# Seven block products for eight in the key and query projections of a hybrid GLA and dilated-window trunk, with low parts added by transfers

## The chip, the cores and the metric

The kernel runs on one core of one Trainium2 chip, as one program. The metric is the device time in microseconds, from the first to the last instruction with what lies around them, as the median of several runs. Engines are named as in the profile: PE is TensorE's matmuls, PEld its weight loads, DVE the VectorE, ACT the ScalarE, POOL the GpSimd and SP the SyncE, which in the kernel before issues all DMA transfers.

## The reference, cut to what matters

A sequence of 1024 tokens with 1024 features goes through two layers. The first is gated linear attention. The second is attention in dilated windows: three groups g with windows of 128, 512 and 2048 tokens at steps of 1, 4 and 16, two key heads c that four query heads each share, and one gate g. The change touches the second layer's projections and how its attention is fed:

```
def shared_kv(x, w_kv):
    kv = x @ w_kv
    k, v = jnp.split(kv, [SWA_KV_HALF], axis=-1)
    k = rope(k.reshape(bsz, s, SWA_N_GROUPS * SWA_KV_HEADS, SWA_HEAD_DIM), pos)
...
def dilated_mixer(x, w_in, w_out, k_sh, v_sh):
    proj = x @ w_in
    q, g = jnp.split(proj, [SWA_Q_TOTAL], axis=-1)
    q = rope(q.reshape(bsz, s, SWA_N_GROUPS * SWA_Q_HEADS, SWA_HEAD_DIM), pos) * (SWA_HEAD_DIM ** -0.5)
    for gi, (window, dilation) in enumerate(SWA_GROUPS):
        o_g, lse_g = dilated_window_attention(q[:, :, gi], k_sh[:, :, gi], v_sh[:, :, gi], window, dilation)
    wts = jax.nn.softmax(jnp.stack(lses, axis=0), axis=0)
    o = jnp.sum(wts[..., None] * jnp.stack(outs, axis=0), axis=0)
    return (o.astype(x.dtype) * jax.nn.silu(g)) @ w_out
...
x = layer_norm(DEEPNORM_ALPHA * x + y, ln_g[layer], ln_b[layer])
```

## The kernel before

**Precision.** Every fp32 product is made of three matmuls in fp32r, a format with a shorter mantissa. A number is split into a high part (`split_hi`, a copy to fp32r) and a low part (`split_lo`, the number less its high part), and `mm3` (L642) adds high by high, high by low and low by high. Tiles with h at the end of their name are high parts, those with l low parts.

**Projections.** `project` (L655) makes one tile of 128 output columns by 1024 tokens: `load_w` (L625) brings 512 KB of weights by SP into `wf` (2 buffers), ACT writes the high part to `wh` (3 buffers), DVE or POOL the low part to `wl` (3 buffers). Then 48 matmuls follow, two halves of 512 tokens by 8 blocks of features by 3. The inputs are x1h and x1l, eight pairs of pages of 128x1024.

**Order of the program.** `layer_a` (from L725) is the first layer. `out_ln` makes its output projection and layer norm for one half of the tokens after the other, and hands on the x1 tiles. `layer_b` (from L1176) then does the following.

1. `proj_v(0)` and `proj_v0` for the first half of the tokens: values for groups 1 and 2, and for group 0.
2. The loop at L1267 to L1270: six key tiles `wK` by `project`, each with `rope` (a product with cosT, two with sinT on 64 rows each, and a sum), and `rows`, which turns one block of x1 through TensorE for the end.
3. `proj_v(1)`, the other values, and the spill of the second key head to DRAM (`kvd`, from L1277).
4. Eight units u, one per query head (loop from L1512): `scores(u)` with masks and exponentials, sums `sts` that go through DRAM and come back turned (`std`, `nat`), the weights of the three groups (`cwd`, `cw`), `q_proj(u + 1)` with three query tiles, `attend(u)`, and the gate tile `g_proj` (L1310) with its product in `close` (L1504). All transfers in this are issued by SP. `reload_kv` brings the second key head after unit 3.
5. `out_ln` and `out_ln_rows` (L1579 to L1595): the output projection and layer norm of the second layer. For the first half of the tokens it is `early()`, within the last units.

**What sets the order.** Nothing is issued where it is written. A list scheduler `Sched` (order from L254, cost from L543) records all operations, estimates each one's time and writes out a fixed order for each engine. `S.later(-WEIGHTS)` lets weight loads go first, `S.later(-EVAC)` lets results leave PSUM early, and an operation given as `S.vp` goes to DVE or POOL, whichever the scheduler finds free first. All instructions are issued at one line (L452 before, L454 after), so they are told apart by tiles. PSUM has four tags of two banks each: acc, lv, po, ms.

Of the kernel before, what the change touches and what calls it, by code (L numbers as in the profile page):

```python
# [7 lines left out]
F32 = mybir.dt.float32  # L8
# [28 lines left out]
RUNS, GATHER = 0.3, 1.0  # L37

# [102 lines left out]
class Sched:  # L141
# [20 lines left out]
    def record(self, engs, meth, args, kw):  # L162
# [10 lines left out]
        if meth == "copy_predicated":  # L173
            ins += outs
# [79 lines left out]
    def order(self):  # L254
# [26 lines left out]
        dma_free = 0.0  # L281
# [35 lines left out]
        while n_done < len(ops):  # L317
# [43 lines left out]
            if e == "SP":  # L361
                dma_free = max(dma_free, st) + c
                o.t1 = dma_free + 1.7
                free[e] = st + 0.37
# [167 lines left out]
def shares_port(e, meth, outs, ins):  # L532

    n = sum(v.buf.pool.space is None for v in ins if int(_np.prod(v.shape[1:])) > 1)
    if e == "POOL":
        return n > 0
# [6 lines left out]
def cost(e, meth, n, outs, ins, args, kw):  # L543
# [14 lines left out]
    if e == "SP":  # L558
        return 0.1 + int(_np.prod((outs + ins)[0].shape)) * 4 / 280e3
# [38 lines left out]
def trunk(tc, xT, wP, wA, wA12, wAv3, w2, wO, wK, wV0, wV12, wB, wOB, par_d,  # L598
# [5 lines left out]
    p0 = S.pool("p0")  # L604
    ps = S.pool("ps", space="PSUM")
# [14 lines left out]

    def hs(half):
# [3 lines left out]
    def load_w(src):  # L625
        with S.later(-WEIGHTS):
            return load_w_now(src)

    def load_w_now(src):
# [9 lines left out]
        split_lo(lo, wf, hi)  # L639
# [15 lines left out]
    def project(piece, xs, evac, halves=(0, 1)):  # L655
        w = load_w(piece)
# [68 lines left out]
    def layer_a(t2, t1, after):  # L725
        lmask = t2.tile([128, NLEV - 2, 32], U8, name="lmask")
        smask = t2.tile([128, 512], F32, name="smask")
# [155 lines left out]
        def gate(h):  # L883
            b = t1.tile([128, T], F32, name="b", tag="b", bufs=2)
            H[h]["b"] = b
            for half in range(2):
# [10 lines left out]
                S.vector.tensor_tensor_scan(b[:, r], smask, mn, 0.0, op0=OP.mult, op1=OP.add)  # L897
# [256 lines left out]
    kvd = [dram.tile([128, T], F32, name=f"kvd{i}") for i in range(4)]  # L1154
# [21 lines left out]
    def layer_b(xs, early):  # L1176
# [12 lines left out]
        cosT = page(p0, F32, "cosT")  # L1189
        S.sync.dma_start(cosT, cos_d)  # L1190
        sinT = page(p0, F32, "sinT")
        S.sync.dma_start(sinT, sin_d)

        def rope(pg, g, half, acc):
# [8 lines left out]
        K = [[page(p0, F32, f"K{c}{g}") for g in range(3)] for c in range(2)]  # L1203
        V = [[None] * 3 for _ in range(2)]

        def proj_v0(blocks):
            for c in range(2):
                if V[c][0] is None:
                    V[c][0] = page(p0, F32, f"V{c}0")

            def evac(j, acc):
                S.scalar.activation(blk(V[0][0], j), acc[:, 0:128], AF.Copy)
                S.vector.tensor_copy(blk(V[1][0], j), acc[:, 128:256])
            project_tok(wV0, xs, [(j, lambda x, j=j: blk(x, j)) for j in blocks], evac)

        def proj_v(half):
# [12 lines left out]
            with S.later(-EVAC):  # L1231
                pgs = [page(p0, F32, "Vn") for _ in range(2)]
# [24 lines left out]
        def rows(et):  # L1257
            f, t = small("x1f", "d", 4), small("x1r", "d", 4)
# [5 lines left out]

        proj_v(0)
        proj_v0(range(4))
        for g in range(3):  # L1267
            for c in range(2):
                project(wK[2 * g + c], xs, lambda hf, acc, p=K[c][g]: rope(p, g, hf, acc))
                rows(2 * g + c)  # L1270
        proj_v(1)
        for g in (1, 2):
            load_v(0, g)
        rows(6)
        rows(7)
        proj_v0(range(4, 8))
        for g in range(3):  # L1277
            S.sync.dma_start(kvd[g], K[1][g])
        S.sync.dma_start(kvd[3], V[1][0])

        def reload_kv():
            for g in range(3):
                K[1][g] = page(p0, F32, f"K1{g}")
                S.sync.dma_start(K[1][g], kvd[g])
            V[1][0] = page(p0, F32, "V10")
            S.sync.dma_start(V[1][0], kvd[3])
            load_v(1, 1)
            load_v(1, 2)


# [12 lines left out]
        def q_proj(u):  # L1303
            Q = [page(p0, F32, "Q") for _ in range(3)]
            U[u]["Q"] = Q
            for g in range(3):
                project(wB[u, g], xs, lambda half, acc: rope(Q[g], g, half, acc))


        def g_proj(u):  # L1310
            sg = page(p0, F32, "sg")
            U[u]["sg"] = sg
# [373 lines left out]
```

## Time and profile before

| | us |
|---|---|
| median of 3 runs | 1154.0 |
| lowest and highest run | 1153.88, 1154.59 |
| span of the profiled execution | 1152.7 |
| PE busy in it | 1142.8 |
| DVE busy | 820.3 |
| ACT busy | 449.1 |
| POOL busy | 188.0 |

Busy times are sums over the instructions of an engine, and the page gives them as shares of the span. The windows of the trace show the same for a stretch, the chain of waits follows the work that ended last back to the start, and groups by form give the mean duration of one instruction of a shape. In a group the number after x is the count, then come the busy time, the mean in ns, and the idle time ahead of it with what ended it. Of the page's issues, these are the ones that the change moves or adds to, with their count and size:

```profile
wf<-in_wB SPq DMA_DIRECT2D x32, 512.0 KB
...
wf<-in_wK SPq DMA_DIRECT2D x6, 512.0 KB
```

The first are the weights of the 24 query tiles and 8 gate tiles, the second those of the six key tiles.

### The profile page before, as it was taken

Reading aid. Unit: us, or ns where it says so; the run is one execution under the profiler, and the core shown is the slowest. Engines: PE = TensorE matmul, PEld = TensorE weight load, DVE = VectorE, ACT = ScalarE, POOL = GpSimd, SP = SyncE. Lnnn points to the kernel's source line nnn. Section 1 sums busy time; section 2 is a strip of 40 time slices with the busy share of each in tenths; the row PEclk is TensorE's granted clock in tenths of the full one; section 3 lists DMA queues with packets and bytes.
Section 4 is the critical chain, followed back from the end, with each engine's and each line's share of the span. In section 5 each row is a group of like instructions: output and inputs, shape, how many; then the busy total and the mean of one; then the engine's idle time right before and its main releaser. Section 6 shows DMA issues by size and latency. Waiting matters only on the chain.

```text
span 1152.7 us, 19731 instructions
## 1 busy us (share of the span) xinstructions
PE 1142.8 (99%) x7780; PEld 975.2 (85%) x7780; DVE 820.3 (71%) x1634; ACT 449.1 (39%) x929; POOL 188.0 (16%) x139
## 2 busy tenths in 40 slices
PE   9999999999999999999999999999999999999997
PEld 9888888889988888888988888888888888888876
DVE  6286862786966699764366868686777878767678
ACT  5355431646463335311214242424222443444342
POOL 1000100112011120211020303030211312212200
PEclk9999999999999999999999999999999999999999
DMA  7211222111144365443611111121141111134544
GB/s 256 71 38 38 74 79 87 38 61 51 57 171 140 137 214 158 166 143 103 208 47 34 51 38 57 38 50 45 38 165 39 38 21 38 39 96 126 193 136 182
DMA packets 93372, 108.39 MB, mean 94 GB/s; under 512 B 43648, under 2 KB 61952, under 8 KB 93280
## 3 DMA queue, kind: packets, MB, share of 16 engines
q1 hardware_dynamic: 93280, 107.13, 29.6%
q8 instruction: 61, 1.00, 0.4%
q14 instruction: 31, 0.25, 0.1%
HBM read 85.94 MB, written 21.17 MB: 93 GB/s over the span
## 4 chain that ended last, share of the span: by engine, by line
PE 93%; DVE 4%; DMA 2%; ACT 1%; issue 1%; POOL 0%; DVEq 0%; ACTq 0%
PE acc L452 63%; PE po L452 9%; PE lv L452 8%; PE vac L452 7%; PE ms L452 4%; PE pro L452 2%; DMA wf<-in_wOB 2%; DVE rt L452 1%; DVE wl L452 1%; DVE x1l L452 0%; ACT wh L452 0%; DVE P L452 0%; DVE lnA L452 0%; ACT woh L452 0%; DVE wol L452 0%
## 5 line engine op out<-in xcount | busy, mean ns | idle before, releaser
L452 PE MATMUL acc<-x1h,wh 128*128 128x512 f32 x608 | 252.3, 415 | 0.0
L452 PE MATMUL acc<-x1h,wl 128*128 128x512 f32 x608 | 237.6, 391 | 0.0
L452 PE MATMUL acc<-x1l,wh 128*128 128x512 f32 x608 | 237.1, 390 | 0.0
L452 ACT ACTIVATE wh<-wf 128x1024 fp32r<-128x1024 f32 (+2 forms) x104 | 108.1, 1040 | 281.0 <-PE acc L452 194.8
L452 POOL TENSOR_TENSOR wl<-wf,wh 128x1024 fp32r<-128x1024 f32 x39 | 93.5, 2397 | 553.1 <-ACT wh L452 414.8
L452 ACT ACTIVATE P<-P,sts 128x128 f32<-128x128 f32 (+2 forms) x192 | 81.5, 426 | 139.6 <-DVE sts L452 139.3
L452 PEld LDWEIGHTS acc<-x1h,wl 128*128 128x128 f32 x608 | 114.1, 188 | 24.5
L452 PEld LDWEIGHTS acc<-x1l,wh 128*128 128x128 f32 x608 | 114.5, 188 | 21.3
L452 PEld LDWEIGHTS acc<-x1h,wh 128*128 128x128 f32 x608 | 114.4, 188 | 21.1
L452 DVE TENSOR_TENSOR wl<-wf,wh 128x1024 fp32r<-128x1024 f32 (+2 forms) x66 | 83.4, 1265 | 58.2 <-ACT wh L452 48.0
L452 PE MATMUL acc<-xh,wh 128*128 128x512 f32 x256 | 101.8, 397 | 0.0
L452 PE MATMUL acc<-xh,wl 128*128 128x512 f32 x256 | 99.8, 390 | 0.0
L452 PE MATMUL acc<-xl,wh 128*128 128x512 f32 x256 | 99.7, 390 | 0.0
L452 DVE TENSOR_TENSOR t<-acc,cosT 128x512 f32<-128x512 f32 x60 | 41.4, 689 | 65.7 <-PE acc L452 65.7
L452 DVE TENSOR_TENSOR t<-acc,sinT 64x512 f32<-64x512 f32 x120 | 82.5, 688 | 1.6
L452 PE MATMUL lv<-K,Q 128*64 128x64 f32 (+2 forms) x512 | 70.2, 286 | 0.0
L452 DVE CUSTOM_DVE_ANT_0 P<-lv,bmask 128x256 f32<-128x256 f32 (+1 forms) x128 | 46.7, 379 | 25.1 <-PE lv L452 23.7
L452 PEld LDWEIGHTS lv<-K,Q 128*128 128x128 f32 (+1 forms) x512 | 53.8, 163 | 10.0 <-issue 1.6
L452 PE MATMUL acc<-ogh,wh 128*128 128x512 f32 x152 | 60.1, 395 | 0.0
L452 PE MATMUL acc<-ogh,wl 128*128 128x512 f32 x152 | 59.2, 389 | 0.0
L452 PE MATMUL acc<-ogl,wh 128*128 128x512 f32 x152 | 59.2, 389 | 0.0
L452 PEld LDWEIGHTS acc<-xh,wl 128*128 128x128 f32 x256 | 48.0, 188 | 10.2
(252 smaller groups left out, 2233.4 us busy)
## 6 DMA issues: line engine op xcount, KB each, us to landing
wf<-in_wB SPq DMA_DIRECT2D x32, 512.0 KB
wf<-in_wA SPq DMA_DIRECT2D x24, 512.0 KB
wf<-in_wO SPq DMA_DIRECT2D x16, 512.0 KB
wf<-in_wOB SPq DMA_DIRECT2D x16, 512.0 KB
wf<-in_wV SPq DMA_DIRECT2D x12, 512.0 KB
res<-in_xT SPq DMA_DIRECT2D x16, 256.0 KB
x1d<-rt SPq DMA_DIRECT2D x16, 256.0 KB
out<-rt SPq DMA_DIRECT2D x16, 256.0 KB
```

Of the source, the lines that this page charges most:

```text
L452: getattr(handle[o.eng], meth)(*[conv(a) for a in args], **{k: conv(v) for k, v in kw.items()})
```

## The change

**Seven products.** Two tiles of 128 columns that read the same x1 form a matrix product of two by two blocks: two tiles by two halves of the features for the weights, two halves of the features by two halves of the tokens for x1. Eight block products, each of 4 x 3 matmuls of 128x512, give the four results. The change uses the scheme with seven: P1 to P7, with four sums of weight blocks (built by `load_pair`) and four sums of x1 blocks, T1 to T4 (built by `sums`, 16 pages of 128x1024). Nine pairs go this way: the three pairs of key tiles, and 12 of the 24 query tiles by the list EARLY, all of it ahead of attention. The results, and the values of group 0, are stored to DRAM (`kd`, `qd`, `vd0`) and loaded when a unit needs them.

```
EARLY = [(0, 1, 2), (2, 3, 2), (0, 2, 1), (4, 5, 2), (6, 7, 2), (4, 6, 1)]
...
                def put(w, x, more=None):
                    hi, lo = w
                    split_hi(hi, x)
                    S.scalar.activation(lo, x, AF.Copy, scale=-1.0)
                    if more is None:
                        S.gpsimd.dma_start(lo, x, accum_op=OP.add)
                    else:
                        S.gpsimd.dma_start(four(lo), more, accum_op=OP.add)
                    return four(hi), four(lo)
...
                w0, w1 = halves()
                a11 = put(w0, a[:, L], src[0][:, 0:4])
                t3 = total(S.vp.tensor_sub, a[:, L], b[:, L])
                s3 = put(w1, t3)
                w0, w1 = halves()
                a12 = put(w0, a[:, R], src[0][:, 4:8])
                a22 = put(w1, b[:, R], src[1][:, 4:8])
                w0, w1 = halves()
                t1 = total(S.vp.tensor_add, b[:, L], b[:, R])
                s1 = put(w0, t1)
                t2 = total(S.vp.tensor_sub, t1, a[:, L])
                s2 = put(w1, t2)
                t4 = total(S.vp.tensor_sub, a[:, R], t2)
                s4 = put([small("s4", "d", 4, FR) for _ in range(2)], t4)
            return dict(P1=a11, P2=a12, P4=a22, P7=s3, P5=s1, P6=s2, P3=s4)
...
        def seven(w, evac):
...
            acc = prod("P1", "a")
            u = small("u1", "a", 13)
            with S.later(-WEIGHTS - EVAC):
                S.scalar.copy(u, acc)
            acc = prod("P7", "b")
            f = small("u2", "a", 13)
            with S.later(-WEIGHTS - EVAC):
                S.scalar.copy(f, acc)
            acc = prod("P2", "a")
            with late():
                evac(0, 0, acc)
            prod("P4", "b")
            acc = prod("P5", "c")
            with late():
                S.vector.tensor_add(f, f, acc)
            acc = prod("P6", "d")
            with late():
                S.vector.tensor_add(u, u, acc)
                c21 = small("c", "a", 13)
                S.vector.tensor_add(c21, u, banks["b"])
                evac(1, 0, c21)
                S.vp.tensor_add(f, u, f)
                evac(1, 1, f)
            acc = prod("P3", "c")
            with late():
                S.vector.tensor_add(u, u, acc)
                evac(0, 1, u)
...
        def sums():
            for k in range(4):
                t, low = raws[k], raws[k + 4]
                old, old2 = (small("old", "d", 4) for _ in range(2))
                S.sync.dma_start(old, x1d[k][:, 0:512])
                S.sync.dma_start(old2, x1d[k + 4][:, 0:512])
                S.vp.tensor_sub(old, t, old)
                keep("T1", k, old)
                S.vp.tensor_sub(t, low, t)
                keep("T3", k, t)
                S.vp.tensor_sub(low, low, old)
                keep("T2", k, low)
                S.vp.tensor_sub(old2, old2, low)
                keep("T4", k, old2)
```

The order of `layer_b` ahead of attention becomes proj_v(0), proj_v0, proj_v(1), proj_v0, sums, nine pairs.

**Low parts by transfers.** In a pair, and in `q_proj` and `g_proj` (`added=True`), the low part is no longer a subtraction on DVE or POOL. ACT writes the negated high-precision number to wl, in fp32r, and a DMA that POOL issues adds the number itself to it: 63 such transfers of 256 KB and 20 of 512 KB.

```
-        split_lo(lo, wf, hi)
+        if added:
+            S.scalar.activation(lo, wf, AF.Copy, scale=-1.0)
+            S.gpsimd.dma_start(lo, src, accum_op=OP.add)
+        else:
+            split_lo(lo, wf, hi)
```

**Rope.** Two copies on ACT and one product take the place of two products on DVE, and the sign in the table of sines is turned.

```
-            S.vector.tensor_mul(t2[0:64, :], acc[64:128, :], sinT[64:128, r])
-            S.vector.tensor_mul(t2[64:128, :], acc[0:64, :], sinT[0:64, r])
+            S.scalar.copy(t2[0:64, :], acc[64:128, :])
+            S.scalar.copy(t2[64:128, :], acc[0:64, :])
+            S.vp.tensor_mul(t2, t2, sinT[:, r])
```

**Units.** The 18 small transfers of a unit (std, nat, cwd, cw) are issued by ACT instead of SP. The exponentials P of group 0 get pages of p0, so that those of two units can be held at once. The gate tile comes after `attend`, and multiplies og directly; `close` is gone. og of units 0 to 5 is stored in halves. The copies of og from PSUM may go to ACT.

```
-                        S.sync.dma_start(nat[i * 64:i * 64 + 64, s, 1, :],
+                        S.scalar.dma_start(nat[i * 64:i * 64 + 64, s, 1, :],
...
-                    p = small("P", "a", 13)
+                    if g:
+                        p = small("P", "a", 13)
+                    else:
+                        if j0 % 4 == 0:
+                            pg = page(p0, F32, "P")
+                        p = pg[:, hs(j0 // 2 % 2)]
...
         for u in range(8):
             scores(u)
-            if u < 4:
-                g_proj(u)
+            if u == 3:
+                reload_k(1)
             if u + 1 < 8:
                 q_proj(u + 1)
             if u < 7:
                 attend(u)
                 if u < 4:
-                    close(u)
+                    g_proj(u)
             if u == 3:
-                reload_kv()
-        for u in (4, 5, 6, 7):
-            if u == 7:
-                early()
+                reload_v(1)
+        for u in (4, 5, 6):
             g_proj(u)
-            if u < 7:
-                close(u)
+        early()
         attend(7)
-        close(7)
+        g_proj(7)
```

**Room and planner.** A pool px of four pages holds cosT, sinT, a pair's results and V. The mask of the scan in the first layer is half as wide, and the scan is made in two halves. The planner keeps one DMA queue per engine, with a cost for POOL's (QUEUED 5.2, ISSUE 0.9).

**How instructions move.** On TensorE, in the first half of a key tile before, x1h and x1l come block by block with weights wh and wl:

```order
L452 MATMUL acc<-x1h_4244,wh 128x512
L452 MATMUL acc<-x1l_4252,wh 128x512
L452 MATMUL acc<-x1h_4244,wl 128x512
L452 MATMUL acc<-x1h_4254,wh 128x512
L452 MATMUL acc<-x1l_4283,wh 128x512
L452 MATMUL acc<-x1h_4254,wl 128x512
```

After the change, the end of P1 and the whole of P7 of the first pair (sev is a bank of a pair, T a page of a sum with its high and low part side by side):

```order
L454 MATMUL sev<-x1h_4335,wh 128x512
L454 MATMUL sev<-x1l_4350,wh 128x512
L454 MATMUL sev<-x1h_4335,wl 128x512
L454 MATMUL sev<-T_4858,wh 128x512 x2
L454 MATMUL sev<-T_4858,wl 128x512
L454 MATMUL sev<-T_4917,wh 128x512 x2
L454 MATMUL sev<-T_4917,wl 128x512
L454 MATMUL sev<-T_5017,wh 128x512 x2
L454 MATMUL sev<-T_5017,wl 128x512
L454 MATMUL sev<-T_5172,wh 128x512 x2
L454 MATMUL sev<-T_5172,wl 128x512
```

A product is 12 matmuls of the same shape, and its four blocks of T take the place of eight blocks of x1.

On POOL, before, around the border of the two layers: x1l are low parts of x1, wl those of weights, twelve of them in a row.

```order
L452 MEMSET diag 128x512 x2
L452 TENSOR_TENSOR lnA<-lnA,rt 128x512
L452 TENSOR_TENSOR x1l_4390<-rt,x1h_4373 128x512
L452 TENSOR_TENSOR x1l_4445<-rt,x1h_4430 128x512
L452 TENSOR_TENSOR wl<-wf,wh 128x1024 x12
```

After, a stretch of about one pair among the nine: sum is a sum of weight blocks, s the low part for P3, in_wB the weights in DRAM, u a result.

```order
L454 DMA wl<-sum 128x512 x2
L454 DMA s_6501<-sum 128x512
L454 DMA wl<-in_wB 128x512
L454 DMA wl<-sum 128x512
L454 DMA wl<-in_wB 128x512 x2
L454 TENSOR_TENSOR u_6519<-u_6496,u_6519 128x512
```

POOL's subtractions there have become issues of adding transfers, one for each product.

On SP, before, the small transfers of one unit (std in DRAM, nat in SBUF, cwd the weights on their way back):

```order
L452 DMA std_5943<-sts 128x2x4 x2
L452 DMA nat<-std_5943 64x1x8 x4
L452 DMA std_5943<-sts 8x16x8 x2
L452 DMA nat<-std_5943 64x8x1 x2
L452 DMA wf<-in_wB 128x1024
L452 DMA nat<-std_5943 64x8x1 x2
L452 DMA cwd_6119<-ew 8x8x8 x4
```

After, the same on ACT in an early unit, between exponentials (P), the high and negated parts of weights (wh, wl) and the copies of rope (t):

```order
L454 DMA std_7028<-sts 128x2x4
L454 ACTIVATE P,sts<-P,sts 128x256
L454 DMA nat<-std_7028 64x1x8
L454 ACTIVATE P,sts<-P,sts 128x256
L454 DMA nat<-std_7028 64x1x8
L454 ACTIVATE P,sts<-P,sts 128x256
L454 ACTIVATE wh<-wf 128x1024
L454 ACTIVATE wl<-wf 128x1024
L454 ACTIVATE t_7081<-acc 64x512 x2
L454 ACTIVATE P,sts<-P,sts 128x256 x4
L454 DMA std_7028<-sts 8x16x8 x2
L454 DMA nat<-std_7028 64x1x8 x2
```

The transfers have left SP and stand between ACT's own instructions, where each waits for the one that it reads from.

More of the change, by code (lines that the diff above doesn't have):

```diff
@@ L360, in order @@
             o.t0, o.eng = st, e
[L361 to L364, printed above, removed]
+            if o.calls[0][0] == "dma_start":
+                queue[e] = max(queue[e], st) + c
+                o.t1 = st + c + QUEUED if e == "POOL" else queue[e] + 1.7
+                free[e] = st + (ISSUE if e == "POOL" else 0.37)
             else:
@@ L1204, in layer_b @@
         V = [[None] * 3 for _ in range(2)]
-        def proj_v0(blocks):
-            for c in range(2):
[L1208 to L1214, printed above, removed]
+        L, R = slice(0, 512), slice(512, 1024)
```

196 lines of the change are left out of this document (134 added, 62 removed).

## The prediction

> **What bounds the kernel now.** I read the page's head first, then the tenths, the chain by engine, and then the stages that the change touches.
>
> ```profile
> span 1152.7 us, 19731 instructions
> PE 1142.8 (99%) x7780; PEld 975.2 (85%) x7780; DVE 820.3 (71%) x1634; ACT 449.1 (39%) x929; POOL 188.0 (16%) x139
> PE   9999999999999999999999999999999999999997
> PEclk9999999999999999999999999999999999999999
> ...
> PE 93%; DVE 4%; DMA 2%; ACT 1%; issue 1%; POOL 0%; DVEq 0%; ACTq 0%
> ```
>
> TensorE is idle for 1152.7 − 1142.8 = 9.9 us in all, its clock is granted in full in every slice, and the chain is 93% TensorE. So the time is the sum of the matmuls, as long as the other engines keep up. Two stages matter: the K and V projections (about 407 to 566 us) and the attention units (605 to 1047 us). Windows of them follow; the columns are length, busy time of PE, PEld, DVE, ACT and POOL with counts, granted clock, DMA share and GB/s.
>
> ```profile
> 407.00:438.00 31.00, 30.63 (x134) 24.77 (x132) 29.24 (x39) 12.24 (x17) 6.79 (x6) 1.00 0.66 214
> 453.00:532.00 79.00, 79.00 (x405) 67.42 (x405) 56.05 (x75) 20.08 (x31) 15.58 (x7) 1.00 0.47 151
> 866.00:1047.00 181.00, 181.00 (x1032) 154.63 (x1031) 139.22 (x395) 71.00 (x225) 41.04 (x36) 1.00 0.20 52
> 1105.00:1153.00 48.00, 40.30 (x199) 33.97 (x198) 41.28 (x72) 19.00 (x32) 1.28 (x1) 0.95 0.41 143
> ```
>
> In the K stage and in attention TensorE is busy all the time. 7.7 of its 9.9 idle us lie in the last 48 us, which the change hardly touches. The chain in order of time (start, length, what, matmuls) gives the price of a tile half and the period of a late unit:
>
> ```profile
> 476.18 10.91 PE acc L452 x48
> 487.09 0.44 PE ms L452 x4
> 487.53 10.92 PE acc L452 x48
> ...
> 889.09 1.50 PE lv L452 x34
> ...
> 939.20 1.50 PE lv L452 x34
> ...
> 989.30 1.50 PE lv L452 x34
> ```
>
> One projected tile is 48 matmuls of 128x512 in 10.91 us: 0.2273 us each. A unit starts every 50.1 us. Its three query tiles are 32.8 of that, the attention proper 17.3.
>
> **Term 1, matmuls removed.** Nine pairs of tiles are computed by seven products of 12 matmuls each: 84 instead of 96 per pair. 9 × 12 = 108 matmuls × 0.2273 = **24.5 us** off a bound engine, and a pair lasts 84 × 0.2273 = 19.1 us. All else on TensorE is only reordered.
>
> **Term 2, do the helpers keep up in a pair's 19.1 us?** Rows by form (busy total, mean ns):
>
> ```profile
> L452 ACT ACTIVATE x1h<-rt 128x512 fp32r<-128x512 f32 x16 | 10.0, 627 | 18.6 <-DVE rt L452 18.5
> L452 ACT ACTIVATE k<-acc 128x512 f32<-128x512 f32 x8 | 4.8, 597 | 10.5 <-PE acc L452 10.4
> L452 ACT ACTIVATE aT<-ms 16x512 fp32r<-16x512 f32 x4 | 2.2, 579 | 0.6 <-DVE aT L452 0.6
> L452 DVE TENSOR_TENSOR t<-acc,cosT 128x512 f32<-128x512 f32 x60 | 41.4, 689 | 65.7 <-PE acc L452 65.7
> L452 DVE TENSOR_TENSOR rt<-rt,R 128x512 f32<-128x512 f32 x24 | 16.0, 683 | 0.3 <-ACT R L452 0.3
> L452 DVE TENSOR_TENSOR Q<-t,t 128x512 f32<-128x512 f32 x40 | 54.6, 1366 | 1.2
> L452 DVE TENSOR_TENSOR K<-t,t 128x512 f32<-128x512 f32 x12 | 17.9, 1491 | 0.4
> L452 POOL TENSOR_TENSOR Q<-t,t 128x512 f32<-128x512 f32 x8 | 11.3, 1411 | 0.0
> ```
>
> ACT: 7 high parts and 7 negations (627 ns, a 128x512 copy to fp32r), two copies out of PSUM (597) and eight 64x512 copies, taken at the 16-row copy's 579 since a narrower one is hardly shorter: 8.8 + 1.2 + 4.6 = 14.6 us. DVE: four products with cosT at 689, four with sinT at 683, four final adds at about 1430, four weight sums and four adds from PSUM at some 690: 2.8 + 2.7 + 5.7 + 5.5 = 16.7 us, 87%, less what POOL takes over. Both fit. The tightest place is a bank that is read and then accumulated into again, with one product of 12 × 0.2273 = 2.73 us between: the longest DVE instruction, 1.49, ahead of an add of 0.69 makes 2.2. It holds, by 0.5 us. I charge 0.1 us a pair, **1 us**. If DVE were one more add late at one such place in each pair, it would be (2.2 + 1.4 − 2.7) × 9 = 8 us.
>
> **Term 3, low parts by transfers.** This is what the trace of before does not show: every transfer goes through one queue and adds nothing.
>
> ```profile
> q1 hardware_dynamic: 93280, 107.13, 29.6%
> ...
> 1072.59 4.41 DMA wf<-in_wOB
> ...
> 1095.24 5.08 DMA wf<-in_wOB
> ```
>
> The two chain rows are plain 512 KB loads. An accumulate of 256 KB may take as little as half of the first, 2.2 us, or twice the second, 10.2. I take 5, near the row of 512 KB, since the operation reads two times 256 KB. There are three buffers of two products each: a buffer is free when its two products end, and is needed after the other five less one for the order, 13.6 us later with five products. Off that go four ACT instructions (2.5) and two issues on POOL (1.2, at twice the 0.6 of the issue rows below): 9.9 us remain. At 5 us all is covered by the matmuls; at 10.2, 0.3 us stands out for three buffers in each of nine pairs, 8 us. I take nothing for it. Below nothing is possible only in what DVE and POOL save on subtractions, which were hidden already.
>
> Traffic: per pair 2 loads and 2 stores of 0.524 MB and seven accumulates of 0.262 MB. Counted once, that is 3.93 MB in 19.1 us, 206 GB/s. What the chip can do I read from two windows above, where share and rate stand together: 151 / 0.47 = 321 and 214 / 0.66 = 324 GB/s. An accumulate may count up to three times (read, read, write): 398 GB/s, 24% too much; 2.2 times is the most that fits. The first three pairs also carry the transposed rows, about 0.52 MB a tile and three tiles a pair.
>
> The Trainium skill, "DMA: Bandwidth & Descriptors", section Rules for kernel authors, says that an accumulating DMA reads its destination and writes it later. By it each accumulate's bytes count at least twice: 302 GB/s, 94% of what fits, and too much in the pairs with rows, which is the rival "crowded pairs" below. No run yet shows it. The same page's fit for POOL-issued transfers (Anatomy of one DMA) would give an estimate of 2.6 us for 256 KB; by it the low parts are covered as in my sum.
>
> **Term 4, the units.** Twelve query tiles come from DRAM, so a unit has 1.5 tiles on average: 17.3 + 1.5 × 10.91 = 33.7 us instead of 50.1. ACT gets more work in less time, issues above all. Groups of ACT in the window from 866 to 1047 us, issue rows of SP (min/median/max ns) and a wait of SP's queue:
>
> ```profile
> L452 ACT ACTIVATE wh<-wf 128x1024 fp32r<-128x1024 f32 x12 | 12.7, 1056 | 23.8 <-PE acc L452 14.1 <-issue 9.6
> L452 ACT ACTIVATE ogh<-ogf 128x512 fp32r<-128x512 f32 x8 | 4.8, 625 | 1.2 <-DMA ogf<-ogB 1.1
> L452 ACT ACTIVATE th<-acc 128x512 f32<-128x512 f32 x8 | 4.7, 591 | 12.0 <-PE acc L452 12.0
> ...
> L452 SPq DMA_DIRECT2D nat<-std x64: 574/614/640, 619.8 to 1032.1; - x64
> L452 SPq DMA_DIRECT2D std<-sts x32: 365/486/621, 617.0 to 1025.8; - x32
> ...
> L452 SPq DMA_DIRECT2D cwd<-ew x32: 565/593/631, 639.5 to 1043.7; - x32
> ...
> L452 SPq DMA_DIRECT2D cw<-cwd x16: 363/383/527, 642.8 to 1046.3; - x16
> ...
> SPq L452 <- DMA std<-sts: 16.9, 19, 2.0
> ...
> SPq L452 <- DMA cwd<-ew: 4.9, 9, 0.8
> ```
>
> Without these three groups ACT does 71.0 − 22.2 = 48.8 us in 181/50.1 = 3.61 units, 13.5 per unit. To it come 1.5 tiles × (1.06 + 1.06 + 4 × 0.58) = 6.7, the copies of og (1.2 where two go to ACT at 0.6), and 18 issues: 8 × 0.614 + 4 × 0.486 + 4 × 0.593 + 2 × 0.383 = 10.0. That is 31.4 us. An issue that waits for the transfer before it now holds exponentials queued behind it: DVE waits for these, and TensorE for their transposes. The wait rows have 16.9 us for std and 4.9 for cwd over eight units, so 21.8/8 = 2.7 a unit; total 34.1 against TensorE's 33.7. Gate tiles of units 4 to 6 can fill, so I charge 0.5 to 0.8 a unit where ACT is level with TensorE, in the last four units: **3 us**. Bounds: nothing if the waits fall in ACT's idle time; with the longest wait, 2.0, four times a unit (8.0), 39.4 us against 33.7, +6 in each of four units, 24 us.
>
> The Trainium skill, same page, section Issuing engines are not separate DMA queues, has it that issuing from another engine saves only sequencer time. By it the 10.0 us of issues buy no faster transfer, only a free SP; the issue rows above neither confirm nor deny it, since all are SP's.
>
> **Term 5, borders.** Ahead of the first pair stand the sums of quarters: 16 additions and 16 subtractions of 128x512, about 0.69 us each on DVE, 22 us less POOL's share. DVE was busy for 29.24 of the 31 us ahead of it (first window above). Beside the sums TensorE has V to do, now all in one piece: 96 matmuls of 128x512, 21.8 us, and the half-width V0 behind. So DVE is just hidden; P7 reads the first sum 2.73 us after a pair begins. At the other end K and the first queries come back from DRAM into pages that P7 of the last pair gives free, five products or 13.6 us ahead of its end, and a query tile of 10.91 us follows; a load lands in 4.41. Both ends can be had for nothing; if DVE is late with the sums by its own V copies (some 8 of 0.6), it is 5 us. I take **2 us**.
>
> **The sum.** 1152.7 − 24.5 + 1 + 3 + 2 = 1134.2 us of span. The profiled execution lies 1.3 under the median of the runs (1154.0, from 1153.88 to 1154.59), so I forecast **1135 us**, 1.6% under it.
>
> **Rivals.**
> - Waits cost nothing: 1154.0 − 24.5 = 1129.5, with a little saved at the tail 1127 to 1131. For it: the idle time of TensorE is so small now, with DVE at 71%. Against it: ACT is level with TensorE. Chance 0.18.
> - Crowded pairs: accumulates counted twice, with rows and sums in the first three: (5.77 + 1.57) MB / 321 GB/s = 22.9 us, 3.7 over 19.1; some 10 us for those, 1145. Or landings near 10.2: 1143. For it: nothing in the trace says that an accumulate is as cheap as a load. Chance 0.14.
> - ACT becomes the bound in the units: +24 instead of +3 gives 1156 at worst, no change; half of it 1145. For it: the 10 us of issues; against it: the scheduler can put gate tiles between. Chance 0.10, half of it within 0.2% of the time before.
> - Slower: accumulates counted three times saturate the transfers. 7.6 MB / 321 GB/s = 23.7 us a pair, 4.6 over 19.1, nine times +41, from a factor of 2.2 on; net 1171. For it: the window of 407 to 438 us shows the present transfers at 0.66 without any accumulate, so room for 1.8 MB of them per pair is not plenty. Against it: a factor of 3 takes reading the target to cost as much as reading the source, with no overlap of the two. Chance 0.08.
> - The change doesn't do what it says: if TensorE stood for one helper per pair as long as a product lasts, 9 × 2.73 = 24.6 us, the seventh product saved would be given back in waits and the time stay at 1154. The ACT case and this one are one in their sum, and their chance is counted there.
>
> **How the numbers follow.** My forecast (1131 to 1142) has 0.50, the cheap end 0.18, crowded pairs 0.14, the ACT bound 0.10, saturation 0.08. From 1127 to 1154 lie all but saturation, half of the ACT bound and the outer edges of the others, some 0.83. A measurement of this kernel tells about 0.2% (2.3 us) from no change: faster is under 1151.7. That is 0.50 + 0.18 + 0.14 + 0.05 = 0.87; same 0.05; slower 0.08.
>
> **What would show it.** Term 1: chains of 12 matmuls in 2.73 us, and 1.0 in PEclk with TensorE at 99% through the pairs; wrong if gaps before P5 or P7 show "DMA wl". Term 3: the landing of an accumulate, and the DMA share of the pairs: 0.64 if counted once, 0.94 if twice. Term 4: the period of a late unit, 34 us or 40, and waits of PE for ACT's P or for std. Term 5: a gap before the first scores. The forecast falls if TensorE's busy time doesn't drop by 24 to 25 us, or if its idle time rises by more than 15.

## The result and the profile after

The changed kernel takes 1188.4 us (median of 4 runs, 1187.3 to 1196.1) against 1154.3 before: 1.0303 times as long, 95% interval 1.0273 to 1.0334. It is slower by 34 us, where 1135 us were forecast.

The head of the page, its tenths and its queues after the change:

```profile
span 1185.9 us, 20180 instructions
...
PE 1140.4 (96%) x7672; PEld 963.8 (81%) x7672; DVE 809.3 (68%) x1666; ACT 607.5 (51%) x1214; POOL 207.1 (17%) x210
...
PE   9999999999999999968999999999998999999997
...
PEclk9999999999999999989999999999999999999999
...
q1 hardware_dynamic: 61664, 125.61, 32.7%
q0 software_dynamic: 11952, 27.01, 13.1%
q10 hardware_dynamic: 38528, 0.40, 1.8%
...
wl<-in_wB POOLq DMA_DIRECT2D x20, 512.0 KB, 7.9
...
wl<-sum POOLq DMA_DIRECT2D x27, 256.0 KB, 5.1
```

TensorE has 108 matmuls fewer, yet its busy time falls by 2.4 us only, and its idle time rises from 9.9 to 45.5. Most of both has one reason, shown below: it stops, and after some stops it works for a while at half its clock. Two windows of the trace after, the nine pairs and the units (same columns as before):

```profile
501.00:707.00 206.00, 186.47 (x789) 150.39 (x788) 129.21 (x174) 127.67 (x222) 68.44 (x75) 0.95 0.84 204
708.00:1060.00 352.00, 335.57 (x2013) 285.05 (x2012) 227.00 (x795) 192.01 (x572) 76.04 (x90) 0.99 0.46 105
```

**The ledger.** I compare stretches with the same work. The pairs last 206.4 us from their first matmul to the first behind them; 756 matmuls at 0.2273 and eight turned blocks at 0.44 make 175.3: 31.1 lost. Ahead of them, 501.2 us stand against 497.9 before (the end of keys and values, 566.9, less six key tiles and the blocks): 3.3 lost. Behind them, 478.3 stand against 585.8 less twelve tiles at 10.92, 454.8: 23.5 lost. Together 57.9, less the 24.5 gained, makes 33.4, which is the span's growth of 33.2 but for rounding. The waits of PE in the pairs:

```profile
PE sev L454 <- ACT u L454: 10.7, 4, 5.9
PE ms L454 <- DMA x1f<-x1d: 8.3, 3, 3.3
PE sev L454 <- DMA wl<-sum: 0.3, 1, 0.3
```

TensorE hardly waits for an added low part. It waits for ACT's copies of PSUM and for the loads of the turned rows. The first stop, in order of time: SP's issues, then DVE, ACT and PE (start, length, what, and in brackets the idle time ahead with its end):

```profile
502.11 1.71 SPq L454 DMA_DIRECT2D wf<-in_wK  x2
...
510.79 1.29 DVE L454 TENSOR_TENSOR sum<-wf 128x512 f32<-128x512 f32 x2 [3.02 <-DMA wf<-in_wK]
...
511.51 0.63 ACT L454 ACTIVATE wh<-sum 128x512 fp32r<-128x512 f32 x1 [3.17 <-DVE sum L454]
512.05 0.61 ACT L454 ACTIVATE wl<-sum 128x512 fp32r<-128x512 f32 x1
512.57 1.06 ACT L454 ACTIVATE u<-sev 128x512 f32<-128x512 f32 x2
...
513.20 0.79 PE L454 MATMUL sev<-x1h,wh 128*128 128x512 f32 x1 [5.85 <-ACT u L454]
...
514.22 0.63 PE L454 MATMUL sev<-x1h,wl 128*128 128x512 f32 x1
514.64 0.63 PE L454 MATMUL sev<-x1h,wh 128*128 128x512 f32 x1
```

The weights of the next pair, issued at 502.1, are there at 510.8. DVE's sum waits for them, ACT's split for the sum, and the copies that empty P1's bank stand behind that split on ACT. P2 needs the bank, so TensorE stops for 5.85 us. When it goes on, its matmuls start 0.43 us apart (514.22, 514.64) instead of 0.23, for about 5 us.

In the units one example shows ACT's order at work over the small transfers (chain of waits in order of time):

```profile
917.96 5.71 DMA std<-sts
...
924.35 0.51 ACT P L454
...
926.10 0.55 ACT t L454
...
927.35 4.60 PE acc L454 x12
```

ACT stands at the round trip of std, the exponential and rope's copies come after, and TensorE resumes with 12 matmuls in 4.60 us instead of 2.73. The next section shows that the adding transfers have little part in these two examples and make other stops.

### The profile page after: what moved, and what is told of

Read it like the earlier page. It is cut to its first block, busy times and chain, and to the rows that moved or that the text cites. A ratio compares the mean times of both kernels' runs of the same rounds, so it can differ in the third digit from the quotient of the medians.

```text
span 1185.9 us, 20180 instructions
## 1 busy us (share of the span) xinstructions
PE 1140.4 (96%) x7672; PEld 963.8 (81%) x7672; DVE 809.3 (68%) x1666; ACT 607.5 (51%) x1214; POOL 207.1 (17%) x210
## 3 DMA queue, kind: packets, MB, share of 16 engines
q0 software_dynamic: 11952, 27.01, 13.1%
## 5 line engine op out<-in xcount | busy, mean ns | idle before, releaser
L454 ACT ACTIVATE wh<-wf 128x1024 fp32r<-128x1024 f32 (+3 forms) x113 | 105.8, 937 | 152.6 <-PE acc L454 87.6
L454 PE MATMUL acc<-x1h,wh 128*128 128x512 f32 x320 | 140.3, 439 | 2.5 <-ACT t L454 2.5
L454 PE MATMUL acc<-x1h,wl 128*128 128x512 f32 x320 | 127.1, 397 | 0.0
L454 PE MATMUL acc<-x1l,wh 128*128 128x512 f32 x320 | 126.3, 395 | 0.0
L454 PE MATMUL sev<-T,wh 128*128 128x512 f32 x288 | 90.9, 397 | 3.0 <-ACT u L454 2.8
L454 PEld LDWEIGHTS acc<-x1h,wh 128*128 128x128 f32 x320 | 61.1, 191 | 13.4 <-ACT t L454 3.3
L454 PEld LDWEIGHTS acc<-x1h,wl 128*128 128x128 f32 x320 | 60.8, 190 | 13.6
L454 PEld LDWEIGHTS acc<-x1l,wh 128*128 128x128 f32 x320 | 61.3, 191 | 10.4
L454 PEld LDWEIGHTS sev<-T,wh 128*128 128x128 f32 x288 | 54.6, 191 | 15.8 <-ACT u L454 3.7
L454 PEld LDWEIGHTS po<-PT,V 128*128 128x128 f32 x432 | 52.9, 195 | 5.6 <-DVE PT L454 3.8
```

The lines of the kernel that those rows point to most:

```text
L454: getattr(handle[o.eng], meth)(*[conv(a) for a in args], **{k: conv(v) for k, v in kw.items()})
```

## The experiments

Theory A: the adding transfers load the transfer engines, so that other loads land late, and engines that work in a fixed order pass the delay on to TensorE. Rivals: the written order alone, ACT holding the small transfers, POOL's issues. Times in the table are medians; "behind" is the stretch from the end of the pairs to the last matmul, 470.9 us in the changed kernel.

| kernel | us | against before, interval | pairs | behind |
|---|---|---|---|---|
| changed | 1188.4 | 1.0273 to 1.0334 | 206.4 | 470.9 |
| eighth | 1147.5 | 0.9919 to 0.9954 | 184.6 | 455.6 |
| plain | 1153.2 | 0.9984 to 1.0029 | 186.3 | 457.9 |
| small_sp | 1182.8 | 1.0199 to 1.0281 | 207.2 | 467.5 |
| eighth_sp | 1154.2 | 0.9989 to 1.0011 | 183.5 | 460.8 |
| sub_pairs | 1166.7 | 1.0064 to 1.0136 | 182.5 | 473.2 |
| sub_qg | 1173.9 | 1.0139 to 1.0198 | 202.6 | 461.0 |
| sub_all | 1156.7 | 1.0013 to 1.0039 | 181.9 | 461.2 |
| sub_all_sp | 1160.5 | 1.0032 to 1.0072 | 181.6 | 467.4 |
| mixed | 1171.3 | 1.0110 to 1.0176 | 196.0 | 463.3 |
| hold | 1181.7 | 1.0159 to 1.0314 | 200.2 | 474.7 |
| bus | 1202.9 | 1.0404 to 1.0464 | 214.8 | 479.4 |
| late | 1181.7 | 1.0220 to 1.0280 | 181.8 | 488.1 |

**Same order, less traffic (eighth).**

```
-                        S.gpsimd.dma_start(lo, x, accum_op=OP.add)
+                        S.gpsimd.dma_start(lo[56:72], x[56:72], accum_op=OP.add)
```

> The changed kernel with the same order of instructions on every engine, but each adding transfer moves only 16 of 128 partitions (the low parts on the other partitions stay negated numbers, so that part of the computation is left out). Theory A (traffic: the adding transfers fill the transfer engines, share 0.84 in the nine pairs, and the weight loads of the next pair land late; ACT stands at a split behind them and holds back the copies of PSUM): the pairs shrink from 206 us to 176 to 182 and the span from 1186 to about 1155 to 1162. Theory B (the written order alone: loads are issued late because buffers come free late): the pairs stay within 200 to 206 us and the span above 1178. Theory C (POOL's ring of descriptors, which holds two or three transfers): POOL's waits of 3 to 4 us ahead of an issue stay where the transfers are small only if they are per transfer and not per descriptor.

The planner's estimate of an adding transfer is raised eightfold here, so that every engine's order stays the same. 41 us are gone by the medians, in the profiled executions 21.8 of the 31.1 in the pairs and 15.3 of the 23.5 behind them. Theory A holds for the greater part. The sizes were not met: the pairs take 184.6 us, more than the 176 to 182 forecast, and the span is 1148.4, less than 1155 to 1162. The window of the pairs has the transfer engines at 0.52:

```profile
501.00:684.00 183.00, 178.22 (x783) 145.23 (x782) 128.43 (x172) 127.47 (x222) 60.38 (x74) 0.98 0.52 150
```

With the same order, each stop can be found again in the other kernel. Both examples above remain. The first stop, 5.85 us, is 4.10 here and 5.84 in the kernel `plain` below (eighth first, then plain):

```profile
511.03 0.80 PE L454 MATMUL sev<-x1h,wh 128*128 128x512 f32 x1 [4.10 <-ACT u L454]
```

```profile
512.93 0.79 PE L454 MATMUL sev<-x1h,wh 128*128 128x512 f32 x1 [5.84 <-ACT u L454]
```

The stop in the units, 2.47 us, is 1.97 and 2.44. So these two come mostly with the written order and the other loads, and the adding has little part in them. The other six stops of over 1 us in the pairs, 13.1 us in all, are the ones that go: 0.3 us are left of them here and 1.1 in plain. One of them in the changed kernel, from the issue of the weights to TensorE:

```profile
640.57 1.63 SPq L454 DMA_DIRECT2D wf<-in_wB  x2
...
649.85 1.29 DVE L454 TENSOR_TENSOR sum<-wf 128x512 f32<-128x512 f32 x2 [3.63 <-DMA wf<-in_wB]
...
652.68 0.63 ACT L454 ACTIVATE s<-sum 128x512 fp32r<-128x512 f32 x1 [4.53 <-DVE sum L454]
653.22 0.58 ACT L454 ACTIVATE u<-sev 128x512 f32<-128x512 f32 x1
...
653.85 0.50 PE L454 MATMUL sev<-x1h,wh 128*128 128x512 f32 x1 [2.06 <-ACT u L454]
```

And the same place in eighth:

```profile
620.79 1.38 SPq L454 DMA_DIRECT2D wf<-in_wB  x2
...
627.84 1.28 DVE L454 TENSOR_TENSOR sum<-wf 128x512 f32<-128x512 f32 x2
...
633.33 0.39 PE L454 MATMUL sev<-x1h,wh 128*128 128x512 f32 x1
```

With the full traffic DVE waits 3.63 us for the weights and starts its sum 9.28 us after their issue; with an eighth it starts after 7.05 us, without a wait, and TensorE doesn't stop. So 9.3 us of the loss in the pairs, most of it around the first stop, and 8.2 behind them remain with this order and an eighth of the traffic.

**Same bytes, no adding (plain).**

```
-                        S.gpsimd.dma_start(lo, x, accum_op=OP.add)
+                        S.gpsimd.dma_start(lo, x)
```

> The changed kernel with the same order of instructions on every engine, but POOL's 83 transfers copy the number over the negated one instead of adding to it (the low part is then the whole number, so that step of the computation is left out). In the changed kernel POOL's queue moves 27.0 MB in 13.1% of the span, 174 GB/s, and SP's 125.6 MB in 32.7%, 324 GB/s. If it is the adding that costs (the target is read as well), POOL's queue falls to about 7 to 8% of the span, and the loss to between the changed kernel's and that with an eighth of the bytes: span 1155 to 1172. If it is POOL's way of issuing, or the bytes alone: POOL's queue stays near 13% and the span near 1186.

POOL's queue and a landing in this kernel, in the view of transfers:

```profile
q0 software_dynamic: 11952, 27.01, 7.5%
...
wl<-in_wB POOLq DMA_DIRECT2D x20, 512.0 KB, 5.1
```

POOL's issues of one kind in the groups (count, total, mean ns), this kernel first and then the changed one:

```profile
L454 POOL DMA_DIRECT2D wl<-sum x27 | 14.7, 544 | 11.9 <-DVE sum L454 6.4 <-ACT wl L454 2.5 <-ACT V L454 2.3
```

```profile
L454 POOL DMA_DIRECT2D wl<-sum x27 | 24.6, 911 | 31.8 <-issue 17.0 <-ACT t L454 7.5 <-ACT wl L454 3.4
```

27.01 MB take 7.5% of 1152.8 us, 312 GB/s, where adding took 13.1% of 1185.9, 174 GB/s: adding costs 1.80 times a copy in the transfer engines' time. The span of 1152.8 lies a little under the 1155 to 1172 forecast. The bytes alone cost some 6 us (1153.2 against 1147.5), the adding 35.

An issue takes POOL 0.54 us instead of 0.91, so this kernel alone could not tell adding from issuing. The kernel with an eighth of the bytes can:

```profile
L454 POOL DMA_DIRECT2D wl<-sum x27 | 21.6, 890 | 8.7 <-DVE sum L454 3.6 <-ACT wl L454 3.0 <-ACT V L454 2.0
```

Its issues are nearly as long, 0.89 us, and the loss is gone. The length of POOL's issues is not the cause. POOL's idle time ahead of them falls with the traffic, from 31.8 us to 8.7.

**Adding transfers taken out, in pairs, in units and in both (sub_pairs, sub_qg, sub_all).** The edit in the pairs; in the units `added=True` is dropped:

```
-                    S.scalar.activation(lo, x, AF.Copy, scale=-1.0)
-                    if more is None:
-                        S.gpsimd.dma_start(lo, x, accum_op=OP.add)
-                    else:
-                        S.gpsimd.dma_start(four(lo), more, accum_op=OP.add)
+                    split_lo(lo, x, hi)
```

> Only in the nine pairs the low parts are subtractions again (by DVE or POOL); query and gate tiles of the units keep their adding transfers. If traffic is what the pairs lose to (theory A): DVE has 16.7 + 7 x 0.69 = 21.5 us per pair, less what POOL takes (2.4 us each), so the pairs are between 176 and 193 us long and the span 1156 to 1173. If it is the written order (theory B): the pairs stay near 206 us, or longer, as DVE is fuller.

> The pairs keep their adding transfers; only the query and gate tiles of the units have subtracted low parts. With sub_pairs (1166.7) and sub_all this makes a table of two by two. If the adding transfers cost where they run: the pairs stay at 206 us, the units fall by 5 to 15 us, span 1173 to 1183.

> No adding transfers at all, the 18 small transfers of a unit on ACT as in the changed kernel. The two kernels with an eighth of the bytes showed ACT issues 6.6 us better than SP issues. If that holds here: 1152 to 1156, against 1160.5 with SP. If ACT's issues are better only with the adding transfers there: 1160 or more.

The table of two by two: 1188.4 with both, 1166.7 without them in the pairs, 1173.9 without them in the units, 1156.7 without any. They cost where they run: 17 to 22 us by the pairs, 10 to 15 by the units.

**Fewer of them (mixed).** Sums by subtraction, three plain quarters of each pair by adding, none in the units:

```
                     if more is None:
-                        S.gpsimd.dma_start(lo, x, accum_op=OP.add)
+                        split_lo(lo, x, hi)
```

> As sub_all, but of the seven low parts of a pair the three plain quarters of weights are made by adding transfers again (27 of 63), the four sums by subtraction. Dose: seven a pair 206 us, none 182 us. If the adding transfers cost in proportion: 192 us for the pairs, span 1164 to 1168. If they cost only where the transfer engines come near full (share 0.82 to 0.84 with seven, 0.71 with seven plain ones and little lost): pairs 180 to 185 us, span 1150 to 1158.

That the loss sets in only near full transfer engines falls for the mean over the pairs. It is only 0.59, and still 14 of the 24 us are back, more than in proportion (192 forecast, 196.0 found). A wait of PE and the window of the pairs:

```profile
PE ms L454 <- DMA x1f<-x1d: 9.7, 3, 3.8
```

```profile
503.00:690.00 187.00, 173.56 (x752) 140.66 (x752) 143.52 (x201) 104.11 (x182) 38.64 (x39) 0.97 0.59 161
```

Here the loads of the turned rows come late. Issued together with two loads of weights and two adding transfers, the first is waited for until 8.6 us after its issue; at the same place in sub_all it is used after 5.9, without a wait (SP's issue and PE's use; mixed first, then sub_all):

```profile
520.75 0.97 SPq L454 DMA_DIRECT2D x1f<-x1d  x2
...
529.33 1.11 PE L454 MATMUL ms<-ident,x1f 128*128 128x128 f32 x4 [2.75 <-DMA x1f<-x1d]
```

```profile
520.58 0.90 SPq L454 DMA_DIRECT2D x1f<-x1d  x2
...
526.49 0.60 PE L454 MATMUL ms<-ident,x1f 128*128 128x128 f32 x4
```

From 525 to 530 us the transfer engines are nearly full in mixed, 0.96, and at 0.42 in sub_all (the last column but one; mixed first):

```profile
525.00:530.00 5.00, 2.25 (x10) 1.64 (x10) 4.33 (x7) 1.61 (x3) 0.00 (x0) 0.93 0.96 296
```

```profile
525.00:530.00 5.00, 5.00 (x28) 4.17 (x27) 4.84 (x8) 2.67 (x5) 0.39 (x1) 1.00 0.42 156
```

So it is the burst at the start of a pair that counts here, and not the mean. The two kernels were planned apart, and part of the 14 us may come from another order.

**ACT's order (hold, bus).** `hold` makes the planner put ACT's splits of the next pair behind the copies of PSUM; `bus` gives it one queue for all transfers, with an adding one 1.86 times as dear:

```
+            if o.behind:
+                deps.update(o.behind)
...
-                queue[e] = max(queue[e], st) + c
+                bus = max(max(queue.values()), st) + (1.86 * c if e == "POOL" else c)
+                queue[e] = bus
```

> The changed kernel, whole, with its full adding traffic; only the planner is made to put ACT's splits of a next pair behind the two copies of PSUM of the pair before, so that a late load can't hold the copies. If a late load stops TensorE through ACT's order: the stops behind the copies (10.7 us and the half clock after them) go, the pairs fall from 206 to 190 to 198 us, the span to 1172 to 1181. If the late load stops TensorE by itself (weights not ready): the stops come back as waits for weights ahead of P1, P7 or P2, pairs at 203 us or more.

> The changed kernel, whole; only the planner's estimate differs: one queue for the transfers of all engines instead of one each, and an adding transfer costs 1.86 times a plain one. The traffic is the same; in most pairs ACT's two copies of PSUM now stand ahead of the splits of sums that wait for the next weights. If the written order turns late loads into stops of TensorE: the stops behind ACT's copies (10.7 us in the pairs) and behind the rows' loads (8.3 us) fall by more than half, the pairs to 188 to 196 us, the span to 1165 to 1177. If late loads stop TensorE in any order: pairs over 200 us, span over 1180.

In `hold` the stops behind ACT's copies are gone, and the pairs take 200.2 us, 6 less, which lies between its two forecasts. Its two runs are 7 us apart (1178.2 and 1185.3), so the gain in the whole is uncertain. Waits for the rows' loads remain (10.5 us), so ACT's order is one way by which late loads reach TensorE, not the cause. `bus` is 14.5 us slower than the changed kernel and came out on the side of "late loads stop TensorE in any order". But its plan did not do what it was meant to: the copies still stand behind splits, and PE waits for them eight times, 23.6 us. It decides nothing about the cause, since everything else was reordered too.

**Small transfers back on SP (small_sp, eighth_sp, sub_all_sp).**

```
-                    S.scalar.dma_start(dst[1, s].rearrange("(n p r) -> p n r", n=2, r=4),
+                    S.sync.dma_start(dst[1, s].rearrange("(n p r) -> p n r", n=2, r=4),
```

> Only the 18 small transfers of a unit go back from ACT to SP; the order in the pairs stays as it is. Theory A (ACT stands at the round trip through DRAM, 5.7 us at one place, and holds exponentials and copies): the 24 us that the units lose fall to 5 to 10, span 1167 to 1173. Theory B (the units lose to something else, the adding transfers or the late queries): the span stays within 1180 to 1190.

> As the kernel with an eighth of the added bytes, and the 18 small transfers of a unit on SP as well (the low parts on 112 partitions stay negated numbers: that part is left out). With the traffic nearly gone the kernel with ACT issues is at 1147.5. If ACT's holding costs by itself: 1140 to 1145. If it costs only because the transfers that it waits for are late: 1145 to 1150.

> No adding transfers at all (subtractions everywhere), and the small transfers back on SP; seven products, rope by ACT and the spills stay. If the two suspects together are the loss: 31 us in the pairs and 24 us in the units fall to some 10 together, span 1138 to 1148, faster than before. If the spills and reloads of keys and queries, or the stops themselves, are the loss: above 1160.

With the adding traffic SP is better by 5.6 us, without it ACT is better by 3.8 (sub_all) to 6.7 (eighth). That fits issues on ACT that cost by the lateness of what they wait for; since each plan differs, it is not shown more closely. The gains forecast for SP (1167 to 1173 in small_sp, 1138 to 1148 in sub_all_sp) were both missed, and eighth_sp lies above both of its ranges.

**Later landings in the plan (late).**

```
-RUNS, GATHER = 0.3, 1.0
+RUNS, GATHER = 1.5, 2.5
```

> As the kernel without adding transfers and with the small transfers on SP (1160.5), but the planner is told that the small transfers of a unit land 1.2 to 1.5 us later than it was told. If the units' 20 us are lost since the chain of small transfers is longer than planned and TensorE runs into it: 1148 to 1156. If they are lost because the chain of one unit is longer than the work of a unit on TensorE, whatever the order: 1157 to 1163.

A miss: 21 us slower than the same kernel with the old estimates, all of it behind the pairs. The planner's estimate of these landings is no small knob; why this plan is worse was not followed up.

**What the seven products are worth (eight).** Nine pairs as two plain tiles each, at the same place:

```
+            for x, pg in zip((a, b), pgs):
+                project(x[0], xs, lambda hf, acc: rope(pg, g, hf, acc))
```

> As sub_all, but the nine pairs are computed by eight products, two plain tiles each of 48 matmuls of 128x512, with no sums; early order, spills, rope by ACT and all else stay. If the seven products are worth their 24.5 us less the 6 us that a pair stage of 182 us still loses: sub_all is 17 to 20 us faster than this one, this one at 1170 to 1176. If the sums and the fuller helpers eat the gain: less than 8 us between them.

1171.1 us (1.0115 to 1.0174) against 1156.7: the seven products bring 14.4 of their 24.5 us, less than expected. And the early order without them is 17 us slower than the kernel before.

**Fewer early query tiles (early4, early3, early0).** As sub_all with eight, six or no query tiles ahead of attention:

```
-EARLY = [(0, 1, 2), (2, 3, 2), (0, 2, 1), (4, 5, 2), (6, 7, 2), (4, 6, 1)]
+EARLY = [(0, 1, 2), (2, 3, 2), (4, 5, 2), (6, 7, 2)]
```

> As sub_all (1156.7), but eight instead of twelve query tiles are made ahead of attention (four pairs instead of six); 24 more matmuls of 128x512, 5.5 us. Theory A (the units stop since twelve early tiles leave TensorE too little work beside one unit's chain of waits): the units' loss of some 14 us falls by more than 5.5 us, span 1150 to 1156. Theory B (the units' stops do not depend on how much work stands beside the chain): 1160 to 1164.

> As sub_all with six early query tiles; 36 more matmuls than with twelve, 8.2 us. Theory A: 1148 to 1156. Theory B: 1163 to 1167.

> As sub_all with the key tiles alone by seven products, all query tiles in the units as before the change; 72 more matmuls than with twelve, 16.4 us. Theory A: the units lose next to nothing, and what remains is 8.2 us gained, less some 4 us of sums and 2 us of pairs: 1150 to 1155. Theory B: 1171 to 1175.

1154.9 us (0.9992 to 1.0011), 1157.1 (1.0013 to 1.0039) and 1164.0 (1.0075 to 1.0106). By the ledger above, in the profiled executions, the stretch behind the pairs loses 13.8 us with twelve early tiles, 10.2 with eight, 7.1 with six, 7.7 with none. Each figure is one execution, and those of one kernel differ by up to 8 us (early3, 1153.0 to 1161.1). So about 6 us seem to come from too little work beside a unit's chain, and some 8 from the units' new arrangement whatever the work. Theory A's range was met with eight tiles, missed by 1 us with six and by 9 with none, so neither theory was right alone.

**Rope (early4_rope).** early4 with rope on DVE as before:

> As early4 (1154.9), with rope by two products on DVE as before the change instead of copies on ACT and one product. If ACT is what the units still wait for: 1148 to 1153. If DVE (70% busy in the units, 88% in the pairs) is the tighter one: 1157 or more.

1166.2 us (1.0065 to 1.0132): the pairs grow from 142.7 to 155.9 us, the stretch behind shrinks by 3.7. In this plan ACT's copies are a gain in the pairs; where the remaining 8 us of the units lie stays open. No kernel that computes the whole is measurably faster than the one before.

## Why the prediction was wrong

1. **Matmuls removed, 24.5 us:** the count is right, and the pairs show 12 matmuls in 2.73 us where nothing stops them.
2. **Helpers fit into a pair:** right for their busy time, in sub_all too (181.9 us for nine pairs, 6.6 above the sum). The bank that is read and written again was named as the tightest place, with DVE's load as the danger and 0.5 us of room. It did stop TensorE, but by ACT and by a late load. Of the 5.85 us at its first use most come without the adding too (5.84 in plain, 4.10 in eighth), and the sum had no price for them.
3. **Low parts by transfers, "I take nothing for it":** this step failed. In the same order, cutting the added bytes to an eighth takes back 21.8 us in the pairs and 15.3 behind them. The bounds of the step held: an adding transfer counts 1.80 times, inside the bounds of 1 and 3 and under the 2.2 that fit, and the share in the pairs, 0.84, lies between the 0.64 and 0.94 named; the landing of 256 KB has medians of 4.3 to 8.1 us by kind, inside 2.2 to 10.2; TensorE waited 0.3 us for it. But the step asked whether the sum of bytes fits and whether the low parts come in time, and not what the traffic does to the other loads of the same moment. A pair holds both weight buffers, so the next weights have little slack. The rival "crowded pairs" had the mechanism in part: it priced 10 us where the pairs lost 31.1, because it let a loss begin only above the full rate. The rival "slower" had the direction and, with 1171, the nearer time, but its condition, a factor of 2.2 or more, did not come. The Trainium skill, "DMA: Bandwidth & Descriptors", section Rules for kernel authors, has it that an accumulating DMA reads its destination and writes it later. The 1.80 here fits that, and is less than the 2 that the prediction worked out from it.
4. **Units, 3 us:** 23.5 were lost. That this is the upper bound of 24 is luck: the bound was worked out from ACT's load and its waits, while the runs put 15.3 us of the loss on the adding traffic, and without that traffic the issues were better on ACT than on SP.
5. **Borders, 2 us:** 3.3 found.

The signs that the forecast named for its fall both came: TensorE's busy time fell by 2.4 us instead of 24, and its idle time rose by 35.6. But the gaps stood behind ACT's copies and the rows' loads, and not behind "DMA wl", where they were looked for.

No price stood in the sum for a stop of TensorE beyond its own length. In the pairs the stops, added up over PE's timeline, are 19.5 us, and matmuls that start more than 0.23 us apart lose 10.2 more.

## What to carry to other kernels

When a low-cost engine step becomes a transfer, look first at which loads are issued in the same burst and how long before their use, and only then at the mean share of the transfer engines: a mean of 0.59 hid bursts at 0.96 here. Change the traffic alone with the order held fixed; that one run told more than all replanned ones. Then compare the two stop by stop: the first and longest stop was for the most part not one that the added traffic made. And price a stop of a saturated TensorE with the slow matmuls that can follow it.

## What the runs showed of the hardware

A stop of about 2 us can halve TensorE's pace afterwards, but its length alone does not decide. In the changed kernel a stop of 2.06 us is followed by starts 0.43 us apart, while one of 2.83 us is not followed by half pace:

```profile
653.85 0.50 PE L454 MATMUL sev<-x1h,wh 128*128 128x512 f32 x1 [2.06 <-ACT u L454]
...
655.83 0.63 PE L454 MATMUL sev<-x1h,wh 128*128 128x512 f32 x1
656.26 0.63 PE L454 MATMUL sev<-x1l,wh 128*128 128x512 f32 x1
...
902.17 0.63 PE L454 MATMUL ms<-ident,P 128*128 128x128 f32 x4 [2.83 <-DVE sts L454]
```

The granted clock in the trace shows where the two differ. In the pairs and units the half clock lasts 3.41 us each time (6.83 at the first stop), and its beginnings, 511.40, 531.88, 559.19, 589.91, 654.76 us and three in the units, lie whole multiples of 3.41 us apart. Two such stretches around each stop (the third column from the right is the granted clock):

```profile
651.35:654.76 3.41, 1.35 (x6) 0.80 (x6) 3.34 (x6) 2.08 (x5) 0.04 (x1) 1.00 0.32 56
654.76:658.18 3.42, 3.42 (x10) 2.63 (x9) 2.98 (x5) 3.12 (x7) 2.55 (x3) 0.50 0.66 150
...
900.52:903.93 3.41, 1.76 (x12) 1.62 (x12) 3.06 (x16) 2.14 (x13) 0.00 (x0) 1.00 0.94 226
903.93:907.34 3.41, 3.41 (x28) 3.19 (x26) 1.77 (x8) 1.76 (x7) 0.00 (x0) 1.00 0.37 66
```

The stop of 2.06 us lies whole in one stretch, and the next is at half clock. The longer one is cut by a border and leaves 1.65 us of idle time in the second stretch. Where exactly the line is stays open: of the stretches with 1.5 to 2.0 us idle some were followed by half clock and some not.

The Trainium skill, "TensorE: Matmul & The Clock Gate", Part 1, puts the fall to half clock behind about 3.4 us without work; here 2.06 us were enough.
